# A two-layer diffusion step on one core: the S5 set-up moved ahead of the norm and off GpSimd, the late modulation loads put into weight slots, and the softmax division put behind the value products

## The chip, the cores and the metric

The kernel runs on one core of one Trainium2 chip. A time is the device time of one execution in microseconds. The core's engines are TensorE (PE in the rows, with its weight loads as PEld), VectorE (DVE), ScalarE (ACT), GpSimd (POOL) and SyncE (SP), whose queue issues nearly all DMAs. SBUF holds the working tiles, PSUM the matmul results.

## What is computed

One inference step of a two-layer backbone on 640 tokens: 512 latent tokens (a grid of 8 rows by 64) and 128 prompt tokens, 1024 channels, all in float32. The change lies in layer 0, whose mixer has two head groups on one input projection:

```python
hs = modulate(rmsnorm(xs, g), shift, scale)          # shift, scale, gates: adaLN from silu(c) @ ada_w
proj = h @ w_in                                       # 1024 -> 512 (S5) + 3 x 512 (q, k, v)
# A: bidirectional S5, 32 groups x 64 complex states, per direction
a_bar = exp(a * dt);  b_bar = ((a_bar - 1) / a) * b
h_t = a_bar * h_(t-1) + b_bar @ u_t;  y = real(c @ h) + d * u;  y = gelu(y);  y = y * sigmoid(y @ w_glu)
# B: attention, 8 heads of 64: latent queries see 16 columns x 8 rows of neighbours (with bias) and 128 context keys
p = softmax(s);  out = p @ v
out = concat([y_s5, attn]) @ w_out;  x = x + gate * out;  then norm, SwiGLU, residual
```

Layer 1 (a Mamba-2 mixer and its SwiGLU) and the final norm follow.

## The kernel before

Activations lie channels by tokens. Each product is made of float32r halves: a weight tile of 128 x 1024 is loaded (`wraw`, two buffers), split by ScalarE into `whi` and by VectorE into `wlo`, three buffers each from the pool `wts`, and multiplied in three terms (`gemm`, L287: 48 matmuls of 320 columns for one 128-channel output tile). Blocks of 2592 floats come from a pool of twelve (`blk`). A scheduler sets each engine's order of instructions from the written order and the data and buffer dependencies; each engine, and the SP queue too, then runs its list in order.

Layer 0's mixer runs so:

1. `ada_stage` (L212) queues sixteen 512 KB tiles of `in_ada_n` for the first two of five modulation units (scale, then shift), with the first projection weight `w0` between the units.
2. `mixer_input` squares x, runs `ada_unit(1)`, makes the reciprocal norm (L345 on VectorE, then transposes to PSUM and `rext`), multiplies the eight tiles of x by `rext`, even ones on VectorE and odd ones on GpSimd, scales them on ScalarE (L1155), runs `ada_unit(0)`, and then makes `xh` (L1161, ScalarE) and `xl` (L1162, VectorE), which need the shift.
3. `s5_params` makes the S5 powers from small tiles (its first part fills VectorE's idle time early on), loads `s5b` (1 MB), forms `bst` on VectorE and `bsw` on GpSimd, the powers `s5pw`, and the tables `qr, qi, pa, pb, co`, one direction on ScalarE and the other on GpSimd.
4. `s5_input_maps` (three 128 x 1024 products per unit, then transposes, L944) and `s5_output_maps` (three 128 x 1152 products per unit, then small matmuls, L981) build the S5 chunk operators. The first three output units and one input unit are on GpSimd, the rest on VectorE.
5. Four projection tiles give `uT`. `s5_chunks` (L1002, L1010) transposes it, `s5_inject` (L1028) applies the input maps, and `s5_scan` runs 63 serial steps a direction: the backward one on GpSimd, the forward one on VectorE.
6. `attention(p)`, p = 0 to 3, handles two heads each. `scores` puts the scores in PSUM (L1239, L1242), adds the bias and takes the row maximum on VectorE (L1245), exponentiates on ScalarE (L1247), and on VectorE takes the reciprocal of the row sum (L1248) and multiplies the row by it (L1249). `values` transposes the rows (L1256), `outer` multiplies by the values (L1269). For p < 3 the loop also calls `qkv(p + 1)` (three projection tiles) and steps of the forward scan.
7. `attention(3)` is woven with `ada_fill` (modulation units 2, 3 and 4: twelve steps of two 512 KB tiles and four matmuls, L224, all through one block `adaw` that holds one pair at a time; after four steps a copy, L227, and four transposes, L230), with `s5_out` (L1087, L1089, L1098) and with `glu`.

Then come the output projection, the rest of layer 0, and layer 1.

Of the kernel before, what the change touches and what calls it, by code (L numbers as in the profile page):

```python
# [26 lines left out]
BLK = 2592  # L27
# [92 lines left out]
class Kernel:  # L120
# [74 lines left out]
    def ada_stage(self):  # L195
        nc = self.nc
        slot = lambda n: self.wpool.tile([128, 8, 128], F32, name=n).rearrange("p k m -> p (k m)")
        self.scw = [slot("whi" if i % 2 else "wlo") for i in range(6)]
        def two():
            b = self.blk("adak", [BLK])  # L200
            self.adrow.append(b[:, 2048:2560])
            return [b[:, 0:1024], b[:, 1024:2048]]

        self.adrow = []
        self.scw += two()
        large = self.big("adab", [4, 1024])
        self.shw = [large[:, i] for i in range(4)]
        for w, u in ((self.scw, 1), (self.shw, 0)):
            for k in range(8):
                if k == len(w):  # L210
                    w += two()
                nc.sync.dma_start(w[k], self.I["ada_n"][u, k])  # L212
            if u:
                self.w0 = self.raw_w(self.I["ev_w_in"][0], 8)

    def ada_unit(self, u, pair, row):
        nc = self.nc
        ps = self.psum()
# [252 lines left out]
    def ssd_dt(self, ps):  # L471
# [6 lines left out]
        nc.sync.dma_start(par[:, :2], self.I["dtp"])  # L478
        nc.scalar.activation(par[:, 2:3], par[:, 1:2], AF.Exp)
        v.tensor_scalar(par[:, 3:4], par[:, 2:3], -1.0, None, op0=OP.mult)  # L480
        bs = self.small.tile([64, 2], F32, name="dtb", bufs=1)
# [334 lines left out]
    def s5_params(self):  # L816
# [4 lines left out]
        sg = self.sgn  # L821
        b = self.blk("s5b", [2, 64, 16])
        nc.sync.dma_start(b, I["s5b"])
        ring, pin = [0], [3]
# [62 lines left out]
        ts(wi, 1.0, M, 0.0, A, pi[:, 1])  # L887
        f1 = self.blk("s5f1", [BLK])
        f2 = self.blk("s5f2", [BLK])
        self.bst = bst = f1[:, :1040].rearrange("p (g c) -> p g c", c=16)  # L890
        self.pa, self.pb = (f1[:, 1040 + 576 * i:1616 + 576 * i].rearrange("p (g k) -> p g k", k=9) for i in range(2))
        self.bsw = bsw = f2[:, :1024].rearrange("p (g c) -> p g c", c=16)
        self.qr, self.qi = (f2[:, 1024 + 512 * i:1536 + 512 * i].rearrange("p (g k) -> p g k", k=8) for i in range(2))
        v.memset(bst[:, 64:65], 0.0)
        tb = self.blk("s5tb", [2, 64, 16])
        bc = lambda a: a[:, :, None].to_broadcast([128, 64, 16])
        for e, o, x, y, k in ((v, bst[:, :64], b[:, 0], b[:, 1], OP.add), (nc.gpsimd, bsw, b[:, 1], b[:, 0], OP.subtract)):
            w = tb[:, 0 if e is v else 1]
            self.tt(e, o, x, bc(sr), M)
            self.tt(e, w, y, bc(si), M)  # L900
            self.tt(e, o, o, w, k)
        for o0, n, a0, b0 in ((2, 1, 1, 1), (3, 2, 1, 2), (5, 4, 1, 4)):
# [7 lines left out]
            sub(x[0], x[1], pr[:, o0:o0 + n])  # L910
            add(x[2], x[3], pi[:, o0:o0 + n])
        self.co = self.const.tile([128, 2, 2, 2, 32], F32, name="s5co")
        for d in range(2):
            gs = slice(d * 32, d * 32 + 32)
            pk = lambda z: (z[:, ::-1, gs] if d else z[:, :, gs]).rearrange("p k g -> p g k")
            qk = lambda z: (z[:, 0:8, gs] if d else z[:, 7::-1, gs]).rearrange("p k g -> p g k")
            act = lambda o, i, sc: nc.scalar.activation(o, i, AF.Copy, scale=sc) if d == 0 else nc.gpsimd.tensor_scalar(o, i, sc, None, op0=OP.mult)
            act(self.qr[:, gs], qk(pr), 1.0)
# [266 lines left out]
    def ada_fill(self):  # L1185
        blk = self.blk("adaw", [BLK])

        def pair(u):
            def of(i):
                w = [blk[:, a * 1024:a * 1024 + 1024] for a in range(2)]  # L1190
                for a in range(2):
# [4 lines left out]
        for u in (2, 3, 4):  # L1196
            yield from self.ada_unit(u, pair(u), blk[:, 2048:2560])

# [5 lines left out]
    def attention(self, p):  # L1204
# [15 lines left out]
        stat = self.small.tile([128, 2, 2, 5], F32, name="stat")  # L1220
        C = "ctx"
# [4 lines left out]
                (NS, 128, 192, 128, ((0, 128, 3),)))  # L1226
        rc = self.small.tile([128, 2, 5], F32, name="rc")
        pvs = self.mm.tile([128, 2, 512], F32, name="acc")
# [4 lines left out]
        def scores(i):  # L1233
# [9 lines left out]
            for h in range(2):  # L1243
                s, mx, sm = sT(h, i), stat[:, 0, h, i:i + 1], stat[:, 1, h, i:i + 1]
# [38 lines left out]
        o = self.af[:, p]  # L1283
        nc.scalar.activation(o[:, :NS].rearrange("p (r w) -> p w r", r=8), pvs[:, 0].rearrange("p (w r) -> p w r", r=8), AF.Copy)
        nc.scalar.activation(o[:, NS:], pvs[:, 1, :128], AF.Copy)

    def even_mixer(self):
# [3 lines left out]
        self.qkvt, self.rpb = {}, {}  # L1291
        self.s5_params()
        self.s5_output_begin()
        b = self.big("s5e", [4, 8, 8, 16])
        t = self.blk("s5et", [2, 8, 8, 16])
        early = [self.s5_input_maps(4 + i, (t[:, i % 2], b[:, i])) for i in range(4)]
        for _ in self.s5_output_maps(range(0, 3), nc.gpsimd):
            pass
        for m in range(0, 4):
            ps = self.mixer_gemm(m, self.split_w(self.w0, 8) if m == 0 else None)  # L1300
            nc.scalar.activation(uT[:, m, :320], ps[:, 0, :320], AF.Copy)
            nc.scalar.activation(uT[:, m, 320:NS], ps[:, 1, :192], AF.Copy)
# [125 lines left out]
```

## Time and profile before

| | us |
|---|---|
| median of 3 runs | 1998.96 (1998.55 to 2000.91) |
| the profiled execution's own time | 1998.31 |
| its span, first to last instruction | 1996.3 |
| PE busy over the span | 1891.3 (95%) |
| DVE busy over the span | 1262.9 (63%) |

The time exceeds the span by 2.0 us. Busy shares are averages over very different stages; matmul ends are modelled, and a matmul's duration in a row is longer than the distance to the next one.

### The profile page before, as it was taken

To read this page: it belongs to the slowest core of one execution; us is meant where nothing else is said; L and a number is where in the kernel's file an instruction comes from. 1 tells how busy PE (TensorE), PEld (TensorE's weight loads), DVE (VectorE), ACT (ScalarE), POOL (GpSimd) and SP (SyncE) were. 2 spreads that over 40 slices of the span, in tenths; PEclk is the share of its full clock that TensorE was granted. 3 is DMA by queue.
4 is the path that set the end of the run, shared out by engine and by line. 5 is a ranking of instruction groups with operands and counts; after the bars stand their busy time and mean duration, and the time that the engine had idled before them with its cause. 6 is when DMAs were issued, how large, how long until landed. Compare 5 with 4: busy or idle time off the path is not lost.

```text
span 1996.3 us, 30838 instructions
## 1 busy us (share of the span) xinstructions
PE 1891.3 (95%) x12476; PEld 1753.1 (88%) x12476; DVE 1262.9 (63%) x2090; ACT 749.7 (38%) x1238; POOL 439.3 (22%) x451
## 2 busy tenths in 40 slices
PE   4888897899999999999999999998999999999998
PEld 2777773699999999999998788875899999999997
DVE  6979951367864874875878697879645443433434
ACT  5353351343221221233655465655433221221222
POOL 2749810010000000003023535347432000000002
PEclk9988897999999999999999999998999999999999
DMA  7145146544542443433221212123422222222222
GB/s 296 58 130 159 54 139 181 175 151 127 163 144 96 159 151 103 159 109 118 79 74 60 84 59 81 63 75 103 156 75 74 75 74 76 74 67 86 76 62 81
DMA packets 100989, 215.80 MB, mean 108 GB/s; under 512 B 14944, under 2 KB 50416, under 8 KB 100336
## 3 DMA queue, kind: packets, MB, share of 16 engines
q1 hardware_dynamic: 100816, 213.83, 33.6%
q8 instruction: 98, 1.61, 0.3%
q14 instruction: 43, 0.35, 0.1%
q0 software_dynamic: 32, 0.02, 0.0%
HBM read 192.31 MB, written 18.84 MB: 106 GB/s over the span
## 4 chain that ended last, share of the span: by engine, by line
PE 81%; DVE 6%; ACT 2%; DMA 2%; issue 1%; SPq 0%; DVEq 0%; ACTq 0%
PE acc L287 69%; DMA adaw<-in_ada_n 1%; PE pm L450 1%; DVE s5x L182 1%; PE acc L450 1%; PE pm L623 1%; PE pm L690 1%; PE pm L705 1%; PE pm L1089 1%; PE pm L224 1%; DVE cv L556 1%; PE pm L672 1%; DVE mt L182 1%; DVE ssdw L679 1%; PE acc L1269 1%
## 5 line engine op out<-in xcount | busy, mean ns | idle before, releaser
L287 PE MATMUL acc<-xh,whi 128*128 128x322 f32 (+2 forms) x2320 | 553.1, 318 | 6.1 <-ACT xh L1161 4.3
L287 PE MATMUL acc<-xl,whi 128*128 128x322 f32 (+2 forms) x2320 | 550.5, 316 | 1.9 <-DVE xl L1162 1.9
L287 PE MATMUL acc<-xh,wlo 128*128 128x322 f32 (+2 forms) x2320 | 548.2, 316 | 0.0
L186 ACT ACTIVATE whi<-wraw 128x1024 fp32r<-128x1024 f32 (+2 forms) x212 | 221.1, 1043 | 688.7 <-PE acc L287 449.3
L287 PEld LDWEIGHTS acc<-xh,whi 128*128 128x128 f32 (+1 forms) x2320 | 395.2, 191 | 19.3 <-issue 11.2
L287 PEld LDWEIGHTS acc<-xl,whi 128*128 128x128 f32 (+1 forms) x2320 | 396.6, 191 | 12.3 <-issue 9.6
L287 PEld LDWEIGHTS acc<-xh,wlo 128*128 128x128 f32 (+1 forms) x2320 | 394.5, 190 | 10.8 <-issue 10.2
L182 POOL TENSOR_TENSOR ssq<-ssq 128x640 f32<-128x640 f32 (+2 forms) x45 | 71.0, 1578 | 1153.4 <-ACT ssq L321 688.1
L187 DVE TENSOR_TENSOR wlo<-wraw,whi 128x1024 fp32r<-128x1024 f32 (+2 forms) x212 | 268.8, 1268 | 29.8 <-ACT whi L186 28.4
L363 DVE TENSOR_TENSOR ffw<-acc,rext 128x644 f32<-128x644 f32 x88 | 72.9, 828 | 201.5 <-PE acc L287 197.7
L378 DVE SCALAR_TENSOR_TENSOR x<-acc,mod,x 128x320 f32<-128x320 f32 x144 | 54.5, 434 | 163.9 <-PE acc L287 163.9
L243 DVE CUSTOM_DVE_ANT_0 junk<-adar,cond 128x1024 bf16<-128x1024 f32 x112 | 136.8, 1221 | 1.8
L287 PE MATMUL acc<-hh,wlo 128*128 128x320 f32 x592 | 134.5, 309 | 0.0
L287 PE MATMUL acc<-hl,whi 128*128 128x320 f32 x592 | 134.3, 308 | 0.0
L287 PE MATMUL acc<-hh,whi 128*128 128x320 f32 x592 | 134.3, 309 | 0.0
L556 DVE SCALAR_TENSOR_TENSOR cv<-cv,vecs 128x644 f32<-128x644 f32 x96 | 97.7, 1018 | 17.2 <-ACT cv L554 15.7
L287 PEld LDWEIGHTS acc<-hl,whi 128*128 128x128 f32 x592 | 99.0, 188 | 0.0
L287 PEld LDWEIGHTS acc<-hh,whi 128*128 128x128 f32 x592 | 98.9, 188 | 0.0
L287 PEld LDWEIGHTS acc<-hh,wlo 128*128 128x128 f32 x592 | 98.8, 188 | 0.0
L186 ACT ACTIVATE hh<-ffw 128x640 fp32r<-128x640 f32 x44 | 32.5, 739 | 95.4 <-DVE ffw L411 95.4
L287 PE MATMUL acc<-yl,whi 128*128 128x320 f32 x256 | 61.6, 321 | 5.9 <-DVE yl L761 5.9
L679 DVE SCALAR_TENSOR_TENSOR ssdw<-ssdw,dtk,ssdcb 128x128 f32<-128x128 f32 x160 | 58.8, 430 | 11.6 <-ACT ssdw L677 11.3
(356 smaller groups left out, 2783.4 us busy)
## 6 DMA issues: line engine op xcount, KB each, us to landing
adar<-in_ada_w SPq DMA_DIRECT2D x56, 512.0 KB, 4.0
wraw<-in_ffn_w_gate SPq DMA_DIRECT2D x44, 512.0 KB, 3.3
wraw<-in_ffn_w_up SPq DMA_DIRECT2D x44, 512.0 KB, 3.2
wraw<-in_od_w_in SPq DMA_DIRECT2D x40, 512.0 KB, 3.3
wraw<-in_ffn_w_down SPq DMA_DIRECT2D x32, 448.0 KB, 3.4
adaw<-in_ada_n SPq DMA_DIRECT2D x24, 512.0 KB, 3.9
wraw<-in_ev_w_in SPq DMA_DIRECT2D x16, 512.0 KB, 3.6
wraw<-in_ffn_w_down SPq DMA_DIRECT2D x16, 512.0 KB, 3.6
```

Source lines behind the costliest of these rows:

```text
L182: e.tensor_tensor(o, a, b, op=op)
L186: self.nc.scalar.activation(hi, x, AF.Copy)
L187: self.nc.vector.tensor_tensor(lo, x, hi.bitcast(F32), op=OP.subtract)
L224: nc.tensor.matmul(ps[q:q + 32], self.condf[:, 2 * i + a], w[a][:, b * 512:b * 512 + 512], start=i == 0, stop=i == 3)
L243: nc.vector.tensor_tensor_reduce(out=junk, in0=w, in1=self.cond[:, s], scale=1.0, scalar=0.0, op0=OP.mult, op1=OP.add, accum_out=self.mod[ ...
L287: nc.tensor.matmul(ps[:mw, h, :n], a[:, k, :mw], b[:, h * n:(h + 1) * n], start=k0 + k == 0 and q == 0, stop=k0 + k == total - 1 and q == 2)
L363: self.nc.vector.tensor_tensor(t.rearrange("p (h n) -> p h n", h=2), ps[:, :, :GH], self.rext.rearrange("p (h n) -> p h n", h=2), op=OP.mult)
L378: nc.vector.scalar_tensor_tensor(xk[:, a:b], pv, gate[:, m, s:s + 1], xk[:, a:b], op0=OP.mult, op1=OP.add)
L450: nc.tensor.matmul(ps[:, :n], w[:, k], x[:, a:b], start=k == 0 and q == 0, stop=k == nf - 1 and q == 2)
L556: nc.vector.scalar_tensor_tensor(acc, cb[:, k:k + G], cw[:, k * 24 + wi:k * 24 + wi + 1], acc, op0=OP.mult, op1=OP.add)
L623: nc.tensor.matmul(ps, Bt[:, c], xw, start=True, stop=True)
L679: nc.vector.scalar_tensor_tensor(E[:, h], E[:, h], self.dt[:, 0, c, g * 8 + h:g * 8 + h + 1], cbs, op0=OP.mult, op1=OP.mult)
```

## The change

The S5 preparation is cut into a generator. Its first part, with the powers, stands ahead of the squares in `mixer_input`; its second part (tables, all on ScalarE, then `bst` and `bsw`, both on VectorE) stands after the norm. `s5b` is loaded ahead of `w0` and of the shift unit. The x products, all input maps and all output maps are on VectorE; the early maps are written after the four `uT` projections. `ada_fill` takes its tiles from the pool of `whi` and `wlo`, and nine of its twelve steps are woven into attention 0 to 2. In attention, probabilities stay undivided; the ten reciprocals of a head pair are taken at once, spread over channels by ten matmuls against the identity, copied by ScalarE, and multiplied into the value products as these leave PSUM. An exponential of the Mamba stage (`dtp`) is held back to that stage.

```diff
@@ ada_stage
             if u:
+                self.s5b = self.blk("s5b", [2, 64, 16])
+                nc.sync.dma_start(self.s5b, self.I["s5b"])
                 self.w0 = self.raw_w(self.I["ev_w_in"][0], 8)
@@ s5_params (cut)
-        for e, o, x, y, k in ((v, bst[:, :64], b[:, 0], b[:, 1], OP.add), (nc.gpsimd, bsw, b[:, 1], b[:, 0], OP.subtract)):
...
+        yield
-            act = lambda o, i, sc: nc.scalar.activation(o, i, AF.Copy, scale=sc) if d == 0 else nc.gpsimd.tensor_scalar(o, i, sc, None, op0=OP.mult)
+            act = lambda o, i, sc: nc.scalar.activation(o, i, AF.Copy, scale=sc)
...
+        for i, (o, x, y, k) in enumerate(((bst[:, :64], b[:, 0], b[:, 1], OP.add), (bsw, b[:, 1], b[:, 0], OP.subtract))):
+            e, w = v, tb[:, i]
@@ s5_input_maps
-        e = nc.gpsimd if b in (3,) else nc.vector
+        e = nc.vector
@@ mixer_input
+        params = self.s5_params()
+        next(params)
...
-            self.tt(nc.gpsimd if k % 2 else nc.vector, xk, xk, r, OP.mult)
+            self.tt(nc.vector, xk, xk, r, OP.mult)
...
+        next(params)
         for _ in self.ada_unit(0, pairs(self.shw), self.adrow[1]):
@@ ada_fill
-        blk = self.blk("adaw", [BLK])
+        slot = lambda n: self.wpool.tile([128, 8, 128], F32, name=n).rearrange("p k m -> p (k m)")
...
-                w = [blk[:, a * 1024:a * 1024 + 1024] for a in range(2)]
+                w = [slot("whi"), slot("wlo")]
...
-            yield from self.ada_unit(u, pair(u), blk[:, 2048:2560])
+            yield from self.ada_unit(u, pair(u), lambda: slot("whi")[:, :512])
@@ attention
-                nc.vector.reciprocal(rc[:, h, i:i + 1], sm)
-                nc.vector.tensor_scalar(s[:, :n], s[:, :n], rc[:, h, i:i + 1], None, op0=OP.mult)
...
+            if n == 5:
+                nc.vector.reciprocal(rc, stat[:, 1])
+                rp = [self.psum() for _ in range(2)]
+                for i in range(5):
+                    for h, r in enumerate(hs):
+                        nc.tensor.matmul(rp[i // 4][r, i % 4 * 128:i % 4 * 128 + 128], rc[:, i, h:h + 1].to_broadcast([128, 64]), self.ident,
+                                         start=True, stop=True)
...
-        nc.scalar.activation(o[:, NS:], pvs[:, 1, :128], AF.Copy)
+        self.tt(nc.vector, o[:, NS:], pvs[:, 1, :128], rt[:, NS:], OP.mult)
@@ even_mixer
-        for _ in self.s5_output_maps(range(0, 3), nc.gpsimd):
+        for _ in self.s5_output_maps(range(0, 3), nc.vector):
...
+                if i in (3, 7, 11):
+                    next(fill, None)
```

What the scheduler makes of it is seen in the engines' lists. First VectorE between the modulation unit for the scale and the x products, before (`ssq` squares, `mod` modulation, `rs` reciprocal norm):

```order
L182 TENSOR_TENSOR ssq<-ssq,ssq_133 128x640 x2
L234 TENSOR_TENSOR mod_81<-pm,vecs 128x16
L187 TENSOR_TENSOR wlo<-wraw,whi 128x1024
L235 TENSOR_TENSOR mod_81<-pm,mod_81 128x16
L1150 SCALAR_TENSOR_TENSOR amul<-mod_81,vecs 128x16
L345 RECIPROCAL rs<-sd 128x5
L182 TENSOR_TENSOR x<-x,rext 128x640 x4
```

and the same place of the changed kernel (`s5f_318` holds `bst`, `s5f_319` holds `bsw`; `s5e` is an input map's first product):

```order
L182 TENSOR_TENSOR s5f_318<-s5b,s5s 128x1024
L182 TENSOR_TENSOR s5tb<-s5b,s5s 128x1024
L182 TENSOR_TENSOR s5f_319<-s5b,s5s 128x1024
L182 TENSOR_TENSOR s5tb<-s5b,s5s 128x1024
L237 TENSOR_TENSOR mod_81<-pm,vecs 128x16
L182 TENSOR_TENSOR s5f_318<-s5f_318,s5tb 128x1024
L187 TENSOR_TENSOR wlo<-wraw,whi 128x1024
L182 TENSOR_TENSOR s5f_319<-s5f_319,s5tb 128x1024
L238 TENSOR_TENSOR mod_81<-pm,mod_81 128x16
L348 RECIPROCAL rs<-sd 128x5
L1157 SCALAR_TENSOR_TENSOR amul<-mod_81,vecs 128x16
L182 TENSOR_TENSOR x<-x,rext 128x640 x8
```

The six products that need `s5b` stand ahead of the reciprocal norm now, and all eight x products behind it; four `s5e` products and two weight splits follow before the shift unit's `mod`.

Then TensorE at the start of attention(3), before (`adaw` the modulation tiles, `wraw` and `whi` at L1087 and L1089 the S5 output operators):

```order
L1239 MATMUL pm<-attw,qkv 128x128
L1242 MATMUL pm<-qkv 128x256
L1087 MATMUL pm<-wraw,s5u 81x128
L1089 MATMUL pm<-whi,s5x_1121 81x128
L1089 MATMUL pm<-wlo,s5x_862 81x128
L1256 MATMUL pm<-ident,attw 128x128 x2
L224 MATMUL pm<-adaw,condf 32x512 x2
L1269 MATMUL acc<-attb,rpb 64x128 x4
L1269 MATMUL acc<-attb,attw 64x128 x2
L224 MATMUL pm<-adaw,condf 32x512 x8
L230 MATMUL pm<-ident,adaw 128x128 x4
```

and in the changed kernel, where the modulation tiles are `whi` and `wlo`:

```order
L226 MATMUL pm<-whi,condf 32x512 x2
L226 MATMUL pm<-wlo,condf 32x512 x2
L1222 MATMUL pm<-ident,qkv 128x128 x4
L1275 MATMUL acc<-attb,rpb 64x128
L1226 MATMUL pm<-ident,qkv 64x128 x2
L1247 MATMUL pm<-attw,qkv 128x128
L1250 MATMUL pm<-qkv 128x192
L226 MATMUL pm<-whi,condf 32x512 x2
L226 MATMUL pm<-wlo,condf 32x512 x2
L226 MATMUL pm<-wlo,condf 32x512 x2
L233 MATMUL pm<-ident,whi 128x128 x4
L1092 MATMUL pm<-wraw,s5u 81x128
```

Eight of the twelve modulation steps now stand before this place, among the projections of attention 0 to 2; two stand right at its head and two within it.

Behind layer 0's mixer the lists hold the same instructions; a few dozen, all in layer 1, have changed places with near neighbours.

## Rows read from the trace of the kernel before

**Rows 1.** Busy time of each engine by stage of the program.

```profile
core 0: us, PE busy (x) PEld busy (x) DVE busy (x) ACT busy (x) POOL busy (x), PEclk, DMA share, GB/s
0.00:45.00 45.00, 19.66 (x97) 6.13 (x97) 26.70 (x86) 24.68 (x41) 13.32 (x11) 0.96 0.81 301
45.00:113.00 68.00, 55.42 (x362) 52.76 (x362) 59.27 (x66) 23.49 (x52) 47.80 (x19) 0.88 0.31 96
113.00:172.00 59.00, 50.96 (x432) 46.94 (x428) 50.33 (x63) 31.82 (x63) 35.99 (x41) 0.94 0.63 166
172.00:236.00 64.00, 55.45 (x370) 46.68 (x370) 61.15 (x184) 28.80 (x77) 55.28 (x127) 0.89 0.20 68
236.00:289.00 53.00, 51.67 (x348) 43.80 (x348) 34.95 (x126) 22.66 (x67) 17.61 (x43) 0.91 0.36 101
289.00:393.40 104.40, 82.56 (x495) 52.00 (x493) 26.97 (x79) 31.96 (x79) 0.00 (x0) 0.87 0.54 168
393.40:1996.30 1602.90, 1575.53 (x10379) 1504.84 (x10379) 1003.53 (x1490) 586.25 (x863) 269.29 (x212) 0.99 0.31 99
```

**Rows 2.** Chain that ended last, attention(3) stage, 289 to 393.5 us, by line.

```profile
by line: DMA adaw<-in_ada_n 24.1%; PE pm L1089 18.3%; PE pm L224 17.2%; PE pm L1087 8.1%; PE acc L287 5.4%; PE acc L1269 3.9%; PE pm L230 2.8%; PE pm L1242 2.5%; PE pm L1239 2.4%; PE pm L1098 2.2%; PE pm L1256 1.9%; ACT adaw L227 1.7%; issu
```

**Rows 3.** The tile `adaw`: its loads' time from issue to landing.

```profile
DMA to landing us min/median/max: 3.1/3.9/6.5
```

**Rows 4.** Timeline of the first 62 us: start, duration, engine, line, tiles.

```profile
24.00 1.05 PE L224 MATMUL pm<-adak,condf 128*32 128x512 f32 x4 [0.23 <-DMA adak<-in_ada_n]
28.87 0.19 DVE L345 RECIPROCAL rs<-sd 128x5 f32<-128x5 f32 x1 [0.68 <-ACT sd L343]
30.60 7.08 DVE L182 TENSOR_TENSOR x<-x,rext 128x640 f32<-128x640 f32 x4 [1.54 <-ACT rext L357]
30.65 8.43 POOL L182 TENSOR_TENSOR x<-x,rext 128x640 f32<-128x640 f32 x4 [14.38 <-ACT rext L357]
34.25 1.05 PE L224 MATMUL pm<-adak,condf 128*32 128x512 f32 x4 [0.24 <-DMA adak<-in_ada_n]
35.56 1.05 PE L224 MATMUL pm<-adak,condf 128*32 128x512 f32 x4 [0.26 <-DMA adak<-in_ada_n]
44.34 7.33 ACT L1161 ACTIVATE xh<-x,mod 128x512 fp32r<-128x512 f32 x16
45.60 4.45 DVE L1162 SCALAR_TENSOR_TENSOR xl<-x,mod,xh 128x512 fp32r<-128x512 f32 x9
59.56 1.21 DVE L182 TENSOR_TENSOR s5f<-s5b,s5s 128x1024 f32<-128x1024 f32 x1
60.70 1.21 DVE L182 TENSOR_TENSOR s5tb<-s5b,s5s 128x1024 f32<-128x1024 f32 x1
```

**Rows 5.** VectorE, then GpSimd, 55 to 113 us: groups by shape, busy us, mean ns.

```profile
L187 DVE TENSOR_TENSOR wlo<-wraw,whi 128x1024 fp32r<-128x1024 f32 x5 | 12.4, 2481 | 0.0
L182 DVE TENSOR_TENSOR s5et<-s5et,s5e 128x1024 f32<-128x1024 f32 x4 | 10.9, 2722 | 0.1
...
L182 POOL TENSOR_TENSOR s5f<-s5f,s5f 128x1152 f32<-128x1152 f32 x6 | 18.5, 3115 | 0.0
L182 POOL TENSOR_TENSOR s5f<-s5f 128x1152 f32<-128x1152 f32 x3 | 10.8, 3613 | 0.0
```

**Rows 6.** Timeline, S5 transposes to the first scores, on PE, SP and VectorE.

```profile
113.04 2.10 PE L1002 MATMUL pm<-ident,uT 128*81 128x128 f32 x12
...
161.81 0.60 PE L1214 MATMUL pm<-ident,qkv 128*128 128x128 f32 x4
...
171.64 0.49 DVE L1245 CUSTOM_DVE_ANT_0 attw<-pm,rpb 128x320 f32<-128x320 f32 x1 [2.12 <-DMA rpb<-in_rpb]
```

**Rows 7.** Timeline of VectorE and GpSimd where the backward scan starts.

```profile
141.52 5.15 DVE L182 TENSOR_TENSOR s5f<-s5f,s5f 128x1152 f32<-128x1152 f32 x4
143.20 5.48 POOL L182 TENSOR_TENSOR mt<-s5x,s5co 128x128 f32<-128x128 f32 x2 [13.71 <-DMA s5x<-in_s5h]
```

**Rows 8.** VectorE, 172 to 289 us (attention 0 to 2): the softmax division.

```profile
L1249 DVE TENSOR_SCALAR attw<-attw,rc 128x384 f32<-128x384 f32 x12 | 5.8, 483 | 0.0
L1249 DVE TENSOR_SCALAR attw<-attw,rc 128x320 f32<-128x320 f32 x12 | 5.1, 429 | 0.1
L1248 DVE RECIPROCAL rc<-stat 128x1 f32<-128x1 f32 x30 | 4.6, 155 | 1.8 <-ACT attw L1247 1.7
```

**Rows 9.** A run of projection matmuls of the same shape, from the chain.

```profile
407.50 52.52 PE acc L287 x357
```

More of the change, by code (lines that the diff above doesn't have):

```diff
@@ L226, in ada_unit @@
                 yield
+        row = row() if callable(row) else row
         nc.scalar.activation(row, ps, AF.Copy)
@@ L478, in ssd_dt @@
         nc.sync.dma_start(par[:, :2], self.I["dtp"])
-        nc.scalar.activation(par[:, 2:3], par[:, 1:2], AF.Exp)
-        v.tensor_scalar(par[:, 3:4], par[:, 2:3], -1.0, None, op0=OP.mult)
+        with self.behind(nc.scalar, v):
+            nc.scalar.activation(par[:, 2:3], par[:, 1:2], AF.Exp)
+            v.tensor_scalar(par[:, 3:4], par[:, 2:3], -1.0, None, op0=OP.mult)
         bs = self.small.tile([64, 2], F32, name="dtb", bufs=1)
@@ L821, in s5_params @@
         sg = self.sgn
-        b = self.blk("s5b", [2, 64, 16])
-        nc.sync.dma_start(b, I["s5b"])
         ring, pin = [0], [3]
@@ L887, in s5_params @@
         ts(wi, 1.0, M, 0.0, A, pi[:, 1])
[L888 to L896, printed above, removed]
-        for e, o, x, y, k in ((v, bst[:, :64], b[:, 0], b[:, 1], OP.add), (nc.gpsimd, bsw, b[:, 1], b[:, 0], OP.subtract)):
[L898 to L901, printed above, removed]
         for o0, n, a0, b0 in ((2, 1, 1, 1), (3, 2, 1, 2), (5, 4, 1, 4)):
@@ L911, in s5_params @@
             add(x[2], x[3], pi[:, o0:o0 + n])
+        yield
+        f1 = self.blk("s5f1", [BLK])
+        f2 = self.blk("s5f2", [BLK])
+        self.bst = bst = f1[:, :1040].rearrange("p (g c) -> p g c", c=16)
+        self.pa, self.pb = (f1[:, 1040 + 576 * i:1616 + 576 * i].rearrange("p (g k) -> p g k", k=9) for i in range(2))
+        self.bsw = bsw = f2[:, :1024].rearrange("p (g c) -> p g c", c=16)
+        self.qr, self.qi = (f2[:, 1024 + 512 * i:1536 + 512 * i].rearrange("p (g k) -> p g k", k=8) for i in range(2))
+        v.memset(bst[:, 64:65], 0.0)
         self.co = self.const.tile([128, 2, 2, 2, 32], F32, name="s5co")
@@ L924, in s5_params @@
                 act(self.co[:, d, 1, w], pi[:, 8, gs], sg[:, 1 - w:2 - w])
+        tb = self.blk("s5tb", [2, 64, 16])
+        bc = lambda a: a[:, :, None].to_broadcast([128, 64, 16])
+        b = self.s5b
+        for i, (o, x, y, k) in enumerate(((bst[:, :64], b[:, 0], b[:, 1], OP.add), (bsw, b[:, 1], b[:, 0], OP.subtract))):
+            e, w = v, tb[:, i]
+            self.tt(e, o, x, bc(sr), M)
+            self.tt(e, w, y, bc(si), M)
+            self.tt(e, o, o, w, k)
+        yield
     def s5_input_maps(self, b, space=None):
         nc = self.nc
-        e = nc.gpsimd if b in (3,) else nc.vector
+        e = nc.vector
         full = [128, 8, 8, 16]
@@ L1219, in attention @@
         nc.scalar.activation(V[:64, 4:6], ps[:64, :256].rearrange("p (i c) -> p i c", i=2), AF.Copy)
-        stat = self.small.tile([128, 2, 2, 5], F32, name="stat")
+        stat = self.small.tile([128, 2, 5, 2], F32, name="stat")
         C = "ctx"
@@ L1226, in attention @@
                 (NS, 128, 192, 128, ((0, 128, 3),)))
-        rc = self.small.tile([128, 2, 5], F32, name="rc")
+        rc = self.small.tile([128, 5, 2], F32, name="rc")
         pvs = self.mm.tile([128, 2, 512], F32, name="acc")
@@ L1274, in attention @@
                 scores(n)
+            if n == 5:
[5 more added lines that the diff above has]
+                                         start=True, stop=True)
+                rt = self.atts[:, 2:4].rearrange("p b c -> p (b c)")[:, :640]
+                nc.scalar.activation(rt[:, :NS], rp[0], AF.Copy)
+                nc.scalar.activation(rt[:, NS:], rp[1][:, :128], AF.Copy)
             yield
@@ L1283, in attention @@
         o = self.af[:, p]
[L1284 to L1285 removed]
+        wr = lambda z: z.rearrange("p (w r) -> p w r", r=8)
+        self.tt(nc.vector, o[:, :NS].rearrange("p (r w) -> p w r", r=8), wr(pvs[:, 0]), wr(rt[:, :NS]), OP.mult)
+        self.tt(nc.vector, o[:, NS:], pvs[:, 1, :128], rt[:, NS:], OP.mult)
     def even_mixer(self):
@@ L1291, in even_mixer @@
         self.qkvt, self.rpb = {}, {}
-        self.s5_params()
         self.s5_output_begin()
-        b = self.big("s5e", [4, 8, 8, 16])
-        t = self.blk("s5et", [2, 8, 8, 16])
-        early = [self.s5_input_maps(4 + i, (t[:, i % 2], b[:, i])) for i in range(4)]
-        for _ in self.s5_output_maps(range(0, 3), nc.gpsimd):
-            pass
         for m in range(0, 4):
@@ L1303, in even_mixer @@
             nc.scalar.activation(uT[:, m, NS + 8:], ps[:, 1, 192:320], AF.Copy)
+        b = self.big("s5e", [4, 8, 8, 16])
+        t = self.blk("s5et", [2, 8, 8, 16])
+        early = [self.s5_input_maps(4 + i, (t[:, i % 2], b[:, i])) for i in range(4)]
+        for _ in self.s5_output_maps(range(0, 3), nc.vector):
+            pass
         for _ in self.s5_chunks(uT):
@@ L1323, in even_mixer @@
         self.load_bias(0)
+        fill = self.ada_fill()
         for p in range(3):
```

3 lines of the change are left out of this document (1 added, 2 removed).

## The prediction

> **What bounds the kernel now.** I read the busy time of each engine by stage first [rows 1], because the share over the whole span hides the stages that the change touches. Seven stretches: until 45 us the norm; to 113 the four `uT` projections and the S5 maps; to 172 chunks, inject and more maps; to 236 and 289 attention 0 to 2; to 393.4 attention(3) with modulation, S5 output and `glu`; the rest is untouched. TensorE is busy 1575.5 of 1602.9 us in that last one, so only the first 393 us can change much. There PE idles 12.6 us in the second stage, 8.0 in the third, 8.6 in the fourth, where VectorE is busy 61.15 of 64 and so sets the pace, 1.3 in the fifth, where PE does, and 21.8 in the sixth.
>
> The chain of waits of the sixth stage, grouped by line, says what these 21.8 are [rows 2]: 24.1% is the load of `adaw`, 17.2% its matmuls (L224), 2.8% the transposes (L230) and 1.7% the copy (L227). One block holds one pair of tiles, so each load is issued only when the matmuls of the last are done, and lands 3.9 us later at the median [rows 3]. In the second stage the rows of VectorE and GpSimd tell the story [rows 5]: a split of 1024 columns takes 2.48 us and an addition 2.72, where alone a product of this size takes 1.21 and the next starts 1.14 later [rows 4]; GpSimd needs 18.5 + 10.8 = 29.3 us for nine map products.
>
> **A. The front: a loss.** The loads there come one 512 KB tile per 1.3 us (two fours of `adak` matmuls start at 34.25 and 35.56, each behind its tile [rows 4]). `s5b`, 1 MB, now goes ahead of `w0` and the shift unit, so these land 2.6 us later, and `s5b` itself about 2.6 us behind the scale unit's last tile (24.0), at 26.6. The six products that need it stand ahead of the reciprocal norm on VectorE. In-order, they cost six times 1.14, a split as long, and 0.4 for the small ones: the reciprocal starts at 35.0 instead of 28.87. Behind it, as before, 1.7 us pass until x can be multiplied: 36.7. Eight x products on VectorE alone: in proportion to 1.14 for 1024 columns 0.71 each, beside GpSimd 7.08 / 4 = 1.77 [rows 4]; nothing runs beside them now, so I take 0.8, near the first: 6.4, ending at 43.1 where GpSimd ended at 39.1. Four `s5e` products, two splits (six times 1.14) and a small one stand next, then the shift's `mod`, so `xh` starts at about 50.3 instead of 44.34: **6.0 us lost**. By the loads alone it would be 2.6, the lower bound; the upper is 12, if x runs at 1.6.
>
> **B. From there to attention: a gain.** Sixteen `xl` at 4.45 / 9 = 0.49 [rows 4] are 7.9 us, and six maps between them, six times 1.14 and 0.4 more, are 7.3: the last `xl` is done at about 66.2. In the order of instructions 213 projection matmuls stand ahead of the uT transposes, against 282 before; the last `xl` serves the 90th or so. The other 123 at 0.147 (52.52 / 357 [rows 9]) are 18.1; 16 transposes and 24 small matmuls at 2.10 / 12 = 0.175 [rows 6] are 7.0. Transposes of uT then start at 91.3, not 113.04. VectorE keeps up: nine maps from GpSimd are 9 x 1.29 = 11.6 us there (four took 5.15 [rows 7]), and with GpSimd silent its own nine splits and additions shrink by 9 x 1.3 to 1.5, some 12.
>
> The stretch from there to attention's first transposes was 161.81 - 113.04 = 48.8 us [rows 6]. It gains the 69 matmuls left over, 10.1, and loses the waits for maps that stand earlier now; of PE's 8.0 us idle in the stage [rows 1] I take half. So attention starts at 91.3 + 54.9 = 146.2 instead of 161.8: **15.6 us gained, A's loss already in it**. Bounds: 23 if the front hides its loss, 8 if VectorE's maps are late by what PE now no longer waits, and more. The first bias tile ended a wait by 2.1 us at 171.64 [rows 6]; its load goes with the rest.
>
> GpSimd keeps the backward scan, which now starts some 20 us earlier, while VectorE makes its fifteen output maps. Where they met before, VectorE's four products took 1.29 each, unhindered, and GpSimd's two small ones took 5.48 [rows 7]: GpSimd lost, and I count nothing. The Trainium skill ("SBUF — State Buffer", section "Who interferes with whom") says that a VectorE instruction with two SBUF inputs and a GpSimd one that reads SBUF exclude each other and that the one that starts first wins, so VectorE can lose too. By the row the sum stays, and by the rule it is that of the third rival; the trace shows both outcomes, GpSimd losing here and VectorE in [rows 5].
>
> **C. Attention 0 to 2: a small loss.** Removed per head pair on VectorE: (5.8 + 5.1 + 4.6) / 3 = 5.2 us busy [rows 8], 4.3 as durations exceed distances by up to a sixth. Added: two output products of 640 columns together, 0.9, and one reciprocal, 0.2. Net -3.2, which counts in the fourth stage only, as VectorE bounds it alone: two pairs, -6. Added on PE: eight of twelve modulation steps at 1.05 (four matmuls [rows 4]), 8.4; two copies and transposes, (2.8 + 1.7)% of 104.4 / 3 [rows 2] = 1.6 each, 3.2; ten spreading matmuls per pair at 0.175, 5.3. That is 17, of which the idle PE of the fourth stage takes 8, and 9 lengthen the fifth. The modulation loads now wait for a `whi` and a `wlo` slot and are queued on SP between weight loads; behind a late one stands PE's whole list. With three slots each they can be issued well ahead, unlike `adaw`. Nothing in the trace shows this form: between nothing and 8 x 3.9 = 31, I take 4, near nothing. Sum: -6 + 9 + 4 = **7 lost** (bounds 0 and 20, since VectorE's relief and stalls overlap).
>
> **D. Attention(3): a gain.** Out go 24.1 + 17.2 + 2.8 + 1.7 = 45.8% of 104.4, 47.8 us [rows 2]. Back come four steps at 1.05 and one copy with transposes, 5.8, the spreading, 1.8, and waits that lay under `adaw`'s: the first weight tiles of the output side, each some 3.9 us if its slot comes free late. I take 7, near two loads. Left: 104.4 - 47.8 + 14.6 = 71.2, **33.2 gained** (22 if all four steps wait a load and more; 40 with no new wait).
>
> **Rest.** The list of the last stage is the same but for a few dozen near-neighbour swaps: nothing, plus or minus 3, hidden in PE's order.
>
> **Sum.** -15.6 + 7 - 33.2 = -41.8 on a span of 1996.3; with the 2.0 us beside the span 1956.5, say 1956. The profiled execution (1998.31) lies 0.65 below the median and inside its runs' spread, so I do not shift it.
>
> **The rivals.** First, slot sharing stalls PE in attention 0 to 2: eight steps, 3.9 each, 31 us less the 4 counted and some 3 that idle PE hides, 24: 1980. For it: a slot comes free only when a projection's matmuls are done, and SP is in order. Against it: three slots, two thirds of which a projection does not hold at a time. Second, better: the loads hide A (6 us), and no new waits (4 + 7): 1956 - 17 = 1939. For it: PE idle in [rows 1] is larger than the loads need. Third, the backward scan takes VectorE's time: 15 maps x 1.27 (2.48 - 1.21) = 19, less about 10 of slack to PE: 1965. Fourth, slower: every load of all twelve steps exposed, with the SP queue stuck behind it. It decides from an average exposure of (41.8 + 11) / 12 = 4.4 us per step beyond nothing, above the 3.9 median [rows 3] but below its 6.5 maximum; at 5 it gives 2005. Against it: all twelve would have to be as bad as the old single block.
>
> **How the numbers follow.** The forecast (1946 to 1964) has 0.45, slot stalls 0.2, the better case 0.2, the scan 0.1, the slower one 0.05. The range holds all but the tails of the second and fourth: 1935 to 1978. A change under 0.2%, 4 us, is about what a measurement tells from none. Faster by more has 0.92, within it 0.02 (between the first and fourth rival), slower 0.06.
>
> **What would show it.** In the changed kernel's trace: `xh` starting near 50 and the reciprocal near 35 (A); transposes of uT near 91, additions at 1.2 us and attention's first transposes near 146 (B); attention(3) beginning near 280, PE waits named `in_ada_n` on `whi` or `wlo` short (C); none longer than 5 us in attention(3), and the output projection's steady run starting near 351 instead of 393.4 (D); the rest at 1603. It is wrong if loads into `whi` or `wlo` end many of PE's waits before 280, or if the small scan products on GpSimd stand against stretched maps on VectorE.

## The result, and the profile of the changed kernel

The changed kernel takes 1949.4 us (median of four runs, 1947.2 to 1952.7) against 1998.8: a ratio of 0.9752, with an interval of 0.9735 to 0.9769, so 49 us faster. 1956 was forecast, in a range of 1935 to 1978.

Busy time by stage, cut at `xh`, the first transpose of uT, the first transposes of attention(0) and of attention(3), the steady run of the output side, and the end. Unlike [rows 1], which cuts at 172, the third stage ends at attention(0)'s first transposes; 213.0 is only a cut inside attention 0 to 2:

```profile
core 0: us, PE busy (x) PEld busy (x) DVE busy (x) ACT busy (x) POOL busy (x), PEclk, DMA share, GB/s
0.00:53.00 53.00, 21.00 (x97) 8.87 (x97) 41.14 (x122) 28.27 (x51) 4.91 (x7) 0.82 0.72 267
53.00:92.70 39.70, 38.77 (x293) 37.96 (x293) 32.82 (x40) 19.12 (x44) 0.00 (x0) 0.94 0.45 132
92.70:145.20 52.50, 48.32 (x442) 46.63 (x438) 38.21 (x41) 30.76 (x61) 14.17 (x12) 1.00 0.57 145
145.20:213.00 67.80, 56.59 (x391) 42.79 (x387) 64.72 (x176) 24.74 (x69) 59.31 (x137) 0.94 0.47 158
213.00:286.60 73.60, 73.60 (x540) 57.09 (x539) 40.22 (x114) 31.33 (x88) 24.25 (x59) 0.96 0.44 138
286.60:347.80 61.20, 54.71 (x428) 45.79 (x424) 24.16 (x59) 29.16 (x72) 0.00 (x0) 0.98 0.55 149
347.80:1947.20 1599.40, 1572.13 (x10379) 1499.11 (x10379) 1001.10 (x1491) 587.99 (x865) 266.72 (x212) 0.99 0.31 99
```

Against the predicted terms, in us:

| from the start to ... | before | after | change | predicted |
|---|---|---|---|---|
| `xh` | 44.3 | 53.0 | +8.7 | +6.0 (A) |
| attention(0) | 161.8 | 145.2 | -16.6 | -15.6 (A and B) |
| stretch to attention(3) | 127.2 | 141.4 | +14.2 | +7 (C) |
| stretch to the steady run | 104.4 | 61.2 | -43.2 | -33.2 (D) |
| rest | 1602.9 | 1599.4 | -3.5 | 0, within 3 |

The reader should see two things in the stages. GpSimd is silent from 53 to 92.7, and TensorE has 1 us of idle time there where it had 12.6. And the granted clock of attention(3)'s stage is 0.98 of full speed, where [rows 1] has 0.87.

The waits of TensorE in that stage (us in total, times, longest) hold no modulation load any more. First the longest group of the kernel before, then all four of the changed kernel:

```profile
PE pm L224 <- DMA adaw<-in_ada_n: 12.0, 9, 2.7
```

```profile
PE acc L290 <- ACT gh L186: 4.9, 1, 4.9
PE pm L233 <- ACT whi L230: 0.7, 1, 0.7
PE pm L1103 <- ACT s5x L1097: 0.5, 1, 0.5
PE pm L1094 <- DMA whi<-fd: 0.4, 1, 0.4
```

In answer to [rows 5], groups of VectorE from 50 to 113 us: splits and additions take 1.22 us instead of 2.48 and 2.72.

```profile
L187 DVE TENSOR_TENSOR wlo<-wraw,whi 128x1024 fp32r<-128x1024 f32 x7 | 8.6, 1224 | 8.5 <-ACT whi L186 8.5
L182 DVE TENSOR_TENSOR s5f<-s5f,s5f 128x1152 f32<-128x1152 f32 x6 | 8.0, 1355 | 0.0
L182 DVE TENSOR_TENSOR s5et<-s5et,s5e 128x1024 f32<-128x1024 f32 x4 | 4.8, 1222 | 0.0
```

The front, where it lost more than forecast (timeline of ScalarE, TensorE and VectorE):

```profile
25.62 0.64 ACT L913 ACTIVATE s5f<-s5pw 128x256 f32<-128x256 f32 x1 [11.20 <-DVE s5pw L182]
31.20 0.52 ACT L913 ACTIVATE s5co<-s5pw,s5sgn 128x32 f32<-128x32 f32 x2
31.62 0.57 ACT L230 ACTIVATE adak<-pm 128x512 f32<-128x512 f32 x1
32.25 1.12 PE L233 MATMUL pm<-ident,adak 128*128 128x128 f32 x4 [7.29 <-ACT adak L230]
33.16 4.27 PE L344 MATMUL pm<-ones,ssq 128*128 128x1 f32 x20
26.38 1.23 DVE L182 TENSOR_TENSOR s5f<-s5b,s5s 128x1024 f32<-128x1024 f32 x1 [0.47 <-DMA s5b<-in_s5b]
33.40 0.17 DVE L237 TENSOR_TENSOR mod<-pm,vecs 128x16 f32<-128x16 f32 x1 [2.39 <-PE pm L233]
37.76 0.19 DVE L348 RECIPROCAL rs<-sd 128x5 f32<-128x5 f32 x1 [0.69 <-ACT sd L346]
39.96 5.97 DVE L182 TENSOR_TENSOR x<-x,rext 128x640 f32<-128x640 f32 x8 [1.96 <-ACT rext L360]
```

`s5b` and the x products come as worked out (26.38 for 26.6, 5.97 for 6.4). But the reciprocal waits for ScalarE: fourteen S5 tables (L913, 25.6 to 31.7 us) stand ahead of the copy of the scale unit's row (L230), for which TensorE idles 7.29 us. The norm's twenty small matmuls behind that take 4.27 us, at a granted clock of 0.50; before, without such a gap, they took 2.29 at 1.00 (timeline of the kernel before):

```profile
26.24 2.29 PE L341 MATMUL pm<-ones,ssq 128*128 128x1 f32 x20
```

### The profile page after: what moved, and what is told of

Same layout as the page of the kernel before. It is cut to its first block, busy times and chain, and to the rows that moved or that the text cites. A ratio compares the mean times of both kernels' runs of the same rounds, so it can differ in the third digit from the quotient of the medians.

```text
span 1947.2 us, 30947 instructions
## 1 busy us (share of the span) xinstructions
PE 1865.1 (96%) x12556; PEld 1738.2 (89%) x12556; DVE 1242.4 (64%) x2041; ACT 751.4 (39%) x1246; POOL 369.4 (19%) x425
## 4 chain that ended last, share of the span: by engine, by line
PE 83%; DVE 3%; ACT 1%; DMA 1%; issue 1%; DVEq 0%; SPq 0%; ACTq 0%
PE acc L290 71%; PE pm L453 1%; PE acc L453 1%; PE pm L627 1%; PE pm L709 1%; PE pm L1094 1%; PE pm L694 1%; DVE ssdw L683 1%; PE acc L1275 1%; PE pm L676 1%; DVE cv L560 1%; DMA ssq<-yd 1%; PE pm L713 1%; PE pm L226 1%; PE pm L1262 0%
## 5 line engine op out<-in xcount | busy, mean ns | idle before, releaser
L187 DVE TENSOR_TENSOR wlo<-wraw,whi 128x1024 fp32r<-128x1024 f32 (+2 forms) x212 | 263.3, 1242 | 27.6 <-ACT whi L186 26.5
L560 DVE SCALAR_TENSOR_TENSOR cv<-cv,vecs 128x644 f32<-128x644 f32 x96 | 97.9, 1020 | 15.4 <-ACT cv L558 13.8
L683 DVE SCALAR_TENSOR_TENSOR ssdw<-ssdw,dtk,ssdcb 128x128 f32<-128x128 f32 x160 | 60.5, 442 | 11.3 <-ACT ssdw L681 11.0
L182 POOL TENSOR_TENSOR mt<-s5x,s5co 128x128 f32<-128x128 f32 x79 | 42.8, 550 | 119.4 <-ACT s5x L1034 114.5
```

Of the source, the lines that this page charges most:

```text
L182: e.tensor_tensor(o, a, b, op=op)
L187: self.nc.vector.tensor_tensor(lo, x, hi.bitcast(F32), op=OP.subtract)
L560: nc.vector.scalar_tensor_tensor(acc, cb[:, k:k + G], cw[:, k * 24 + wi:k * 24 + wi + 1], acc, op0=OP.mult, op1=OP.add)
L683: nc.vector.scalar_tensor_tensor(E[:, h], E[:, h], self.dt[:, 0, c, g * 8 + h:g * 8 + h + 1], cbs, op0=OP.mult, op1=OP.mult)
```

## The experiments

The theory after the result: the gain is that of the modulation slots and their place (C and D), and of maps that no longer run on GpSimd beside VectorE (B); the softmax is worth nothing; the front's loss comes from ScalarE's tables. Ratios are to the kernel before, run again beside each group of experiments, with their 95% interval; a difference to the changed kernel is the difference of ratios times 1998.8 us, and by the two intervals it is open by some 5 us either way.

**1. Modulation back in one block.** `fill` starts at attention(3) again, with

```
-                w = [slot("whi"), slot("wlo")]
+                w = [blk[:, a * 1024:a * 1024 + 1024] for a in range(2)]
```

> The changed kernel with one part undone: all twelve modulation steps back in attention(3), through the single block adaw. My theory (the load of each pair is exposed because the block holds one pair, and TensorE's clock falls in the gaps): attention(3) takes some 100 us again, attention 0 to 2 get about 12 us shorter, sum 25 to 31 us slower than the changed kernel, 1974 to 1981. Rival (attention(3) is shorter because of the softmax and the earlier start, and the loads would be hidden): within 8 us of the changed kernel, 1950 to 1957.

0.9921 (0.9898 to 0.9943), 1983.7 us: 34 slower than the changed kernel, somewhat over the theory's bracket. The stretch from uT to attention(3) is 10.5 us shorter (183.4 against 193.9), the stage behind it takes 109.4. That stage as a window (columns as above), and its longest wait of TensorE:

```profile
276.30:385.70 109.40, 86.21 (x514) 55.51 (x512) 24.85 (x63) 30.44 (x74) 0.00 (x0) 0.81 0.51 158
```

```profile
PE pm L226 <- DMA adaw<-in_ada_n: 15.4, 12, 2.5
```

**2. Slots, but not earlier.** The tiles stay in the slots of `whi` and `wlo`, but `fill` starts only at attention(3):

```
-                if i in (3, 7, 11):
-                    next(fill, None)
```

> The changed kernel with the modulation steps in the slots of whi and wlo, but all twelve in attention(3). It parts the two halves of that edit. If the deeper buffer is what counts, the waits stay away and the time is 1950 to 1960. If the place counts (the steps' matmuls lie in idle TensorE time of attention 0 and 1, and the weight loads of the S5 output must not share their slots with them), it is 1965 to 1980.

0.9852 (0.9831 to 0.9873), 1970.2 us: 20 slower than the changed kernel, 14 faster than the single block. Both halves count. The same window and waits here:

```profile
277.40:366.50 89.10, 76.72 (x514) 52.38 (x512) 24.24 (x63) 30.25 (x74) 0.00 (x0) 0.92 0.67 203
```

```profile
PE pm L1094 <- DMA whi<-fd: 3.2, 1, 3.2
PE pm L226 <- DMA whi<-in_ada_n: 1.7, 1, 1.7
```

With slots the load waits fall from 15.4 to 1.7 us, TensorE's busy time from 86.2 to 76.7 for the same 514 instructions, and the granted clock rises from 0.81 to 0.92. The earlier place then takes 28 us out of the stage (89.1 to 61.2) and puts about 10 into attention 0 to 2.

**3. The modulation edit alone, on the kernel before.**

```
+                if i in (3, 7, 11):
+                    next(fill, None)
...
-                w = [blk[:, a * 1024:a * 1024 + 1024] for a in range(2)]
+                w = [slot("whi"), slot("wlo")]
```

> The kernel before with only the modulation edit (slots of whi and wlo, nine steps woven into attention 0 to 2). If the parts add up, it gains what undoing it lost, 30 to 35 us: 1964 to 1969. Rival: with the S5 maps and the softmax as before there is less idle TensorE time to take the steps, and it gains 20 to 27: 1972 to 1979.

0.9811 (0.9797 to 0.9826), 1960.3 us: 38 of the 49.6 us (by the ratio) come from this edit alone, more than either theory gave it. With the 16 that the other parts bring without it (experiment 1) that is 54: nearly additive. Part of it comes where nobody looked for it: attention(0)'s first transposes start at 156.6 instead of 161.8.

**4. Softmax as before.** In attention the row's reciprocal and multiplication (L1248, L1249) return, and the ten spreading matmuls go.

```
+                nc.vector.reciprocal(rc[:, h, i:i + 1], sm)
+                nc.vector.tensor_scalar(s[:, :n], s[:, :n], rc[:, h, i:i + 1], None, op0=OP.mult)
```

> The changed kernel with the softmax division as before (reciprocal and multiplication per row block on VectorE, no spreading matmuls). By the terms of the sum VectorE's relief (6 us in the fourth stage) and the matmuls added (5 us, and 1.8 in attention(3)) cancel: within 4 us of the changed kernel, 1946 to 1954. Rival 1, VectorE binds in all of attention 0 and 1: 1956 to 1965. Rival 2, the matmuls and the wait for the last reciprocal cost more than they save: 1938 to 1945.

0.9762 (0.9743 to 0.9781), 1951.8 us: not told apart from the changed kernel, inside the expected bracket. The edit as a whole is worth too little to be measured here; what its two sides, VectorE's relief and the added matmuls, are worth each is not shown by it.

**5. Maps back on GpSimd, in the new order.**

```
-        e = nc.vector
+        e = nc.gpsimd if b in (3,) else nc.vector
...
-        for _ in self.s5_output_maps(range(0, 3), nc.vector):
+        for _ in self.s5_output_maps(range(0, 3), nc.gpsimd):
```

> The changed kernel with the first three output units and input unit 3 back on GpSimd. If GpSimd beside VectorE is what made TensorE wait for maps, additions take about 2.5 us again and the transposes of uT start 5 to 15 us later: 1954 to 1964. Rival (it is the place of the maps behind the projections, not the engine, that counts): within 3 us of the changed kernel.

0.9903 (0.9888 to 0.9917), 1978.8 us: 30 slower, twice the upper end of what was expected. Here the maps meet `xl`. The timeline of GpSimd and VectorE there:

```profile
58.85 15.60 POOL L182 TENSOR_TENSOR s5f<-s5f,s5f 128x1152 f32<-128x1152 f32 x6 [43.44 <-DVE uT L1307]
62.97 9.48 DVE L1170 SCALAR_TENSOR_TENSOR xl<-x,mod,xh 128x128 fp32r<-128x128 f32 x4
```

Four `xl` of 128 columns take 9.48 us, 2.37 each: not much under one GpSimd product (15.60 / 6 = 2.6). In the changed kernel, by group from 52 to 75 us, one takes 0.35:

```profile
L1170 DVE SCALAR_TENSOR_TENSOR xl<-x,mod,xh 128x128 fp32r<-128x128 f32 x8 | 2.8, 346 | 0.0
```

So a short VectorE instruction waits out most of a whole GpSimd one. TensorE waits 11.3 us for `xl`, and uT's transposes start at 110.9 instead of 92.7. That is 18 of the 30 us; 4 more are lost up to attention(0) and 7 within attention 0 to 2, and what causes those was not looked into. The Trainium skill ("SBUF — State Buffer", section "Who interferes with whom") says that the two exclude each other for whole instructions; this row agrees.

**6. Only the maps to VectorE, on the kernel before** (the two lines of experiment 5, the other way).

> The kernel before with only the three early output units and input unit 3 on VectorE, nothing else moved. If what GpSimd costs VectorE is the larger thing, VectorE's splits and additions fall from 2.5 to 1.2 us, the transposes of uT start 6 to 12 us earlier and the time falls by as much: 1987 to 1993. Rival: VectorE's own added 12 us eat what it is relieved of, and it is the early powers and the order that count: 1996 to 2002.

0.9954 (0.9935 to 0.9972), 1988.2 us: 9 faster, inside the first bracket. VectorE's splits and additions take 1.21 us. uT's transposes start at 107.3 instead of 113.0, a little under the 6 us expected, attention(0) at 152.1 instead of 161.8.

**7. Maps written first.** The changed kernel with the block `early = [...]` and the three output units ahead of the loop over the four projections.

> The changed kernel with the early maps written ahead of the four uT projections, as before, still on VectorE. If the written place counts, TensorE waits for maps again and the time is 1954 or more; if only the engine counts, it is within 4 us of the changed kernel, 1945 to 1953.

0.9760 (0.9745 to 0.9775), 1950.0 us: no difference. The written place does not count, because the scheduler gives VectorE the same order of maps, splits and `xl` from it; a list with the maps really ahead was not tried. That the engine counts is what experiments 5 and 6 show.

**8. The products behind the shift unit.**

```
         for _ in self.ada_unit(0, pairs(self.shw), self.adrow[1]):
             pass
+        with self.behind(nc.vector):
+            next(params)
```

> The changed kernel with the six products that need s5b written behind the shift unit and held behind what VectorE was given before them. By the first term of the sum, they delay the reciprocal norm and everything up to xh: xh starts 5 to 8 us earlier (45 to 48 instead of 53) and the time falls by as much, to 1941 to 1945. Rival, the same products then delay xl and the S5 maps, which TensorE needs as soon: xh earlier, but the transposes of uT start where they did, and the time stays at 1948 to 1951.

0.9799 (0.9779 to 0.9818), 1957.5 us: 9 slower. Both brackets missed. The reciprocal still starts only at 38.28, so the products were not what held it. `xh` starts at 51.0, but the products now stand ahead of `xl`, for which TensorE waits 4.3 us, and uT's transposes start at 104.1.

**9. The tables behind `xh`.** They become the last part of the generator:

```
+        with self.behind(nc.scalar):
+            next(params)
```

> The changed kernel with the fourteen S5 tables on ScalarE held behind xh. New theory of the front's loss: in the changed kernel these tables (25.6 to 31.7 us) stand ahead of the copy of the scale unit's row on ScalarE, TensorE idles 7.3 us behind that copy and then runs the norm's matmuls at the lower clock. Then the reciprocal starts at 28 to 31 instead of 37.8, xh at 44 to 47 instead of 53, and the time falls by 6 to 9 us, 1940 to 1943. Rival 1, my prediction's step (the six products on VectorE hold the reciprocal): reciprocal not before 34, xh not before 49, 1946 to 1950. Rival 2: xh is earlier, but the tables now delay the S5 maps and the transposes of uT stay near 92.7: 1948 to 1952.

The new theory is borne out in part, between its bracket and that of the first rival: the reciprocal starts at 33.9, `xh` at 46.6 instead of 53.0, attention(0) at 140.7 instead of 145.2, the steady run at 341.6 instead of 347.8. But the time is 1947.9, 0.9748 (0.9732 to 0.9765), the same as the changed kernel: in the two profiled executions the last stage took 1605.7 instead of 1599.4 us and gave the 6.3 back (below). And uT's transposes did not come earlier (95.3 against 92.7), as the second rival had it; attention(0) gained behind them. With the tables gone, the products do hold the reciprocal, as the prediction had it; this run's timeline of VectorE has no gap between them:

```profile
31.65 1.22 DVE L182 TENSOR_TENSOR s5f<-s5f,s5tb 128x1024 f32<-128x1024 f32 x1
32.78 1.22 DVE L187 TENSOR_TENSOR wlo<-wraw,whi 128x1024 fp32r<-128x1024 f32 x1
33.92 0.19 DVE L348 RECIPROCAL rs<-sd 128x5 f32<-128x5 f32 x1
```

**10. One direction's tables back on GpSimd.** `... if d == 0 else nc.gpsimd.tensor_scalar(...)`, as before.

> The changed kernel with the tables of one direction back on GpSimd, the others still ahead of the copy on ScalarE. By the new theory the copy comes 3 us earlier and the reciprocal 3 to 4 us (about 34): 1944 to 1947. By my prediction's step nothing changes: 1948 to 1951. If GpSimd beside VectorE stretches the six products: slower than the changed kernel.

0.9791 (0.9777 to 0.9806), 1956.7 us: slower, the third bracket, but not for its reason: the six products still take 1.21 us each. The copy comes earlier (TensorE waits 5.3 us for it, not 7.3), yet the products now stand between it and the reciprocal (38.15). The steady run starts 2.7 us later than in the changed kernel, and the last stage, 1605.0, adds 5.6.

**11. Tables behind `xh`, products behind the x products.** Experiment 9 and

```
-        next(params)
+        with self.behind(nc.vector):
+            next(params)
```

> The run with the tables behind xh, and now also the six products that need s5b held behind the eight x products. With the tables gone the products still stood ahead of the reciprocal there (33.9). Theory: the two delays of the front were serial on different engines, and both have to go; the reciprocal starts near 29, xh near 42 (the shift unit's loads land by 39), 4 us earlier than in that run, and the steady run of the output projection starts at 336 to 339; the time is 1941 to 1945 if the last stage costs what it does there, 1935 to 1939 if it is that of the changed kernel. Rival: the products now delay xl and the maps, and attention starts no earlier: 1947 to 1952.

The reciprocal starts at 30.07, but `xh` only at 47.6, and attention(0) at 140.5 as in experiment 9: the products moved on from the reciprocal to the shift unit's `mod`, for which ScalarE waits 4.76 us. The steady run starts at 341.2. 1948.1 us, 0.9751 (0.9732 to 0.977): the rival's bracket, and again the changed kernel's time. No version beat it by more than can be measured.

**12. The changed kernel again.**

> The changed kernel once more, for its last stage. In its profile the stretch from the steady run of the output projection to the end took 1599.4 us, in the kernel before 1602.9, and in the others 1597 to 1606, though only a few dozen instructions have changed places. If the order decides, it comes out within 1 us of 1599.4 again; if it is chance, it comes out anywhere in that band.

0.9751 (0.9736 to 0.9766), and its last stage took 1947.4 - 347.75 = 1599.65 us, with the same list of TensorE: what was expected if the order decides. Chance is not ruled out: the eight executions of this kernel spread over 5.5 us (spans of 1945.4 to 1950.9), nearly as much as the 6.3 in question, and only two of them have a profile. Most of the difference to experiment 9 lies in one 100 us stretch in layer 1's Mamba stage. First the changed kernel's second run, then experiment 9, each from 950 to 1050 us behind its steady run's start:

```profile
1297.75:1397.75 100.00, 88.20 (x495) 67.69 (x495) 74.79 (x111) 51.57 (x83) 60.75 (x41) 0.93 0.42 132
```

```profile
1291.56:1391.56 100.00, 88.07 (x465) 65.75 (x465) 77.47 (x111) 49.85 (x79) 58.52 (x41) 0.90 0.41 130
```

TensorE is as busy, but gets 465 matmuls done instead of 495, at a granted clock of 0.90 instead of 0.93. TensorE's two lists of the last stage differ in 17 places, all in the Mamba stage. Whether one of these swaps does it, and which, was not tried.

## Why the prediction was right, point by point

All four terms moved the way that was forecast: B and D by the mechanism that was named, A by another one, and C with two of its terms mis-sized. That the total came within 7 us is in part luck: C cost 7.2 more than worked out and D gave 10.0 more, and these errors stand against each other.

**A, the front: 6.0 predicted, 8.7 measured, by another mechanism.** The failing step is "the six products that need it stand ahead of the reciprocal norm ... the reciprocal starts at 35.0". They stood there, but it was ScalarE's fourteen tables, called "all on ScalarE" in the change and costed nowhere, that were late last. The copy behind them started 6.5 us later than before (31.62 against 25.10), and the lower clock behind the gap added 2.0 (4.27 against 2.29). The reciprocal came at 37.8; the rest up to `xh` took 15.25 us where 15.3 was worked out. With products taken away alone the reciprocal did not move (experiment 8), with tables taken away it moved by 3.8 us and then stood behind the products (9), with both by 7.7 (11). Two delays lay side by side on two engines.

**B: right, with some luck.** 91.3 was worked out for uT's transposes, 92.7 measured; 146.2 for attention(0), 145.2 measured. But 5 to 7 us of the second figure belong to an edit that B does not count: with the modulation steps back in attention(3), attention(0) starts at 152.0 and 150.1 (experiments 1 and 2), and on the kernel before they alone bring it 5.2 us forward (3). Why they do was not traced. That GpSimd is what cost VectorE is shown by experiments 5 and 6; what the x products, the earlier powers and `dtp` are worth by themselves was not tried. The scan's rival, VectorE losing 1.27 us a map to the earlier backward scan, hardly came. In the changed kernel, GpSimd's small products and VectorE's maps side by side:

```profile
130.64 2.75 POOL L182 TENSOR_TENSOR mt<-s5x,s5co 128x128 f32<-128x128 f32 x2 [114.53 <-ACT s5x L1034]
133.35 3.15 POOL L182 TENSOR_TENSOR s5x<-s5x,mt 128x128 f32<-128x128 f32 x2
134.82 5.96 DVE L182 TENSOR_TENSOR s5f<-s5f,s5f 128x1152 f32<-128x1152 f32 x4 [0.21 <-DMA s5f<-in_s5c]
```

VectorE's four maps take 5.96 where they took 5.15 [rows 7], 0.2 more each; GpSimd's small ones 1.4 to 1.6 each.

**C: 7 predicted, 14.2 measured.** Two terms were mis-sized, both of them idle time of TensorE that was to go. In the kernel before the stretch has these two rows (columns as above):

```profile
161.80:236.00 74.20, 62.54 (x424) 52.71 (x422) 68.99 (x204) 29.65 (x79) 64.70 (x147) 0.91 0.29 95
236.00:289.00 53.00, 51.67 (x348) 43.80 (x348) 34.95 (x126) 22.66 (x67) 17.61 (x43) 0.91 0.36 101
```

TensorE's busy time rose from 114.2 to 130.2 us, near the 17 of added work. But the step "of which the idle PE of the fourth stage takes 8" and VectorE's relief, "two pairs, -6", took 1.8 together: idle time went from 13.0 to 11.2. VectorE's own busy time there did not fall either (103.9 before, 104.9 after), though the division left it: more steps of its scan and two more weight splits lie in the stretch. The longest wait that remains is for the first exponential of attention(0):

```profile
PE pm L1262 <- ACT attw L1255: 6.0, 1, 6.0
```

VectorE takes that block's row maximum only at 159.03, with steps of its scan in its list from 150.15 on; the scores stood in PSUM since 152.6. The stalls on slots, the first rival and 4 us of the sum, did not come: no wait of TensorE on `in_ada_n` shows in attention 0 to 2. Ten modulation steps lie ahead of attention(3)'s first transposes, not eight, and the price of a step was that of half a step: the program's four matmuls of a step leave eight records in the trace (96 in twelve steps), and the row of 1.05 us holds four, those of one tile. A step takes 1.0 us where the records of both tiles run interleaved, 2.1 where one tile follows the other.

**D: 33.2 predicted, 43.2 measured.** "Waits that lay under adaw's ... I take 7" measured 1.6 (0.7 + 0.5 + 0.4 in the list above), two steps remained instead of four, and the clock was left out: the granted clock is 0.87 [rows 1] and 0.81 (experiment 1) with the load waits, 0.92 (experiment 2, with 1.7 us of them left) and 0.98 without. TensorE's busy time in the stage fell from 82.6 to 54.7 us, its idle time from 21.8 to 6.5. C and D together, -29.0 for -26.2, are nearer than either, in part because two steps only changed sides. That 45.8% of a chain leave a stage was too simple a reading, too: of the 24.1% of 104.4 us, 25.2, that the chain puts down to `adaw`'s loads [rows 2], TensorE idled only 12.0; the rest was filled by other matmuls.

**Rest.** Not nothing: -3.5, and 6.3 between the profiles of two kernels whose last stage differs by a few dozen swaps (experiment 12). The step "nothing, plus or minus 3" was too narrow. TensorE's list of layer 1 also differs by more than near neighbours: against the kernel before, some two hundred matmul records of one run of products stand on the other side of smaller ones.

## What to carry to other kernels

Where work moves from one engine to another, read the receiving engine's list around the place where it lands, not only the sender's relief: here fourteen small tables, not six large products, held the chain. A chain's share tells what to remove; how much it frees is TensorE's idle time there, plus what those gaps cost at the lower clock. And where a scheduler orders a whole program, an edit's gain of 5 us can be lost again 1000 us later, in a stage that the edit does not touch, be it by swaps or by chance: compare such kernels by stage, not only by time.

## What the runs showed of the hardware that was not expected

A gap costs TensorE twice. In the kernel before (timeline of TensorE in attention(3)), behind waits for `adaw`, four L224 matmuls that took 1.05 us at the higher clock took 1.92, and pairs of the S5 output (L1089) 0.63 instead of 0.42 to 0.45:

```profile
301.87 1.05 PE L224 MATMUL pm<-adaw,condf 128*32 128x512 f32 x4 [0.92 <-DMA adaw<-in_ada_n]
304.64 1.92 PE L224 MATMUL pm<-adaw,condf 128*32 128x512 f32 x4 [1.72 <-DMA adaw<-in_ada_n]
315.23 0.63 PE L1089 MATMUL pm<-whi,s5x 128*81 128x128 f32 x2
```

The granted clock is 1.00 from 301 to 303 us, and 0.50 from 304.0 to 306.6 and from 313.5 to 317.3: the two levels, 2.4 and 1.2 GHz. For the L224 matmuls the durations come near that ratio; for the pairs they do not (0.43 from one pair to the next against 0.28 later). The second surprise: modulation matmuls of 32 output rows ran two at a time where those of two tiles alternate in the order (eight records in 1.00 us, against four in 0.98 from one tile). Two pieces of the changed kernel's chain in attention(3), start, us, what:

```profile
289.05 1.00 PE pm L226 x8
290.90 0.98 PE pm L226 x4
```
